# The prompt's pick transposes traced among the unsplit u tiles, and one more tile left unsplit

## The chip, the cores and the metric

The kernel runs on one core of a Trainium2 chip. The metric is the device time of one execution in microseconds (us), the lower the better; a version is timed in several runs and its median is compared. Three runs of the kernel before gave 1762.54, 1763.51 and 1766.21 us.

## What is computed

The program is one layer of an encoder for 384 tokens: 128 sample tokens (row tile 0) and 256 prompt tokens (row tiles 1 and 2). The change lies in its last part, a mixture of 16384 tiny experts with product keys:

```python
q = (hb @ w_pq).reshape(PEER_BLOCK, PEER_HEADS, 2, PEER_DHALF)
s = jnp.einsum('nhpd,hpkd->nhpk', q, peer_keys).astype(jnp.float32)
s1, i1 = lax.top_k(s[:, :, 0], PEER_TOPK)
s2, i2 = lax.top_k(s[:, :, 1], PEER_TOPK)
cand = s1[..., :, None] + s2[..., None, :]          # 16 x 16 candidates a head
sc, j = lax.top_k(cand, PEER_TOPK)
e = jnp.take_along_axis(cidx, j, axis=-1)           # cidx = i1 * 128 + i2
g = jax.nn.softmax(sc, axis=-1)
act = jax.nn.gelu(jnp.einsum('nhkd,nd->nhk', peer_u[e], hb))
return jnp.einsum('nhk,nhkd->nd', (g * act), peer_v[e])
```

So every token picks 8 x 16 experts; for each it needs the dot product with a row of `peer_u`, a gelu, the softmax weight `g`, and the sum of rows of `peer_v`.

## The kernel before

The experts are done in two ways. The sample tokens (tile 0) go the sparse way: `peer_sparse` is a Python generator of 128 steps, called *pulls* here. A pull gathers one row of u and v for each token by an indirect DMA that GpSimd issues (L1573, 1 MB into one of `EB` = 3 ring buffers `raw`), takes the dot product on VectorE (L1580), the gelu and the weight on ScalarE (L1581, L1582, `dots`), and adds the v row on VectorE (L1586, `acc`). The prompt tokens (tiles 1 and 2, 256 columns) go the dense way: all 16384 experts in 128 tiles of 128, `dense_u(j)` for gelu(u h) and later `dense_v(j)` for the sum over v. Between the two, `weights(i, T, step)` builds the dense weight matrix from one-hot products (`oh`, L1401, L1448, L1452) out of the picks of tile i and multiplies it into the gelus `G`.

`peer_select(i)` finds the picks. TensorE multiplies with the keys (`dx<-keysT,qp`) into two PSUM banks named `dx`; ScalarE copies to `psc` (L1310). VectorE does the rest: a first stage of maxima, indices and replacements on `psc` (L1314 to L1318), a second on the 80 candidates `pcd` (L1334 to L1338), then bf16 one-hots `poh` (L1358 to L1364) whose sums are the two index tables `pix`, one reduction (L1365) for each half and each four heads; the softmax weights are `pg`. For tiles 1 and 2 the function ends with three TensorE transposes (L1384) of `pix` half 0, `pix` half 1 and `pg` into a `dx` bank, and a ScalarE copy to `pT` (L1386). `weights` starts from `pT`.

A u tile is 128 x 1024 f32 by 256 columns. The first `N1` = 40 tiles are *unsplit*: eight f32 matmuls each (`fx<-h2f,w` and `mm<-h2f,w`, even and odd tiles in the PSUM banks `fx` and `mm`), straight from the loaded tile, with no other engine before them. The later tiles are *split* into two fp32r halves, `wh` by ScalarE (L230) and `wl` by VectorE (L234), and take 24 shorter matmuls (`fx<-h2h,wh` and so on). Up to tile 75 each result goes to `G`.

The program is traced in Python order: selections of tile 0, then tiles 1 and 2, then the unsplit tiles with a half pull for each from tile `S0` = 30 on, then split tiles, weights, and v tiles. A scheduler reorders this and fixes one order for each engine before the run; on the chip each engine works through its list in that order and waits where an operand isn't there. PSUM banks and SBUF buffers rotate by tag (`PSB`: `mm`, `fx`, `dx` two banks, `bx`, `cp` one), so an instruction also waits for the readers of the buffer that it takes over; the tiles of `weights` and the split halves lie in memory that the selection's tiles held. The banks `bx` and `cp` serve the RWKV pairs far ahead and the weights' products later; in between they are free.

Of the kernel before, what the change touches and what calls it, by code (L numbers as in the profile page):

```python
# [176 lines left out]
ORDER = "GGIggggR1R23DMMMGRMRDMRGMGMRMDGMMRRMGDMMMGGGMGGM"  # L177


N1, NW, NA, NB = 40, 76, 8, 24  # L180
SR, UR = (0.5, 0.5, 0.62), 0.5
S0, PH = 30, 4
OFF = [j for j in range(NW, 128) if (j - NW + 1) * NB // (128 - NW) > (j - NW) * NB // (128 - NW)]
# [12 lines left out]
class K:  # L196
# [1099 lines left out]
    def peer_select(self, i, h0=0, nh=8):  # L1296

        nc = self.nc
# [4 lines left out]
        for hb in range(0, nh, 4):  # L1303
            for half in range(2):
                pr = slice(64 * half, 64 * half + 64)
                p = self.ps([128, 4, 128], tag="dx")
# [44 lines left out]
        idx = self.t([128, 2, 8, 16], tag="pix", bufs=2)[:, :, :nh]  # L1351
# [15 lines left out]
        gw = self.t([128, nh, 16], tag=f"pg{i}{h0}", pool=self.pool if i else self.hpool2)  # L1367
# [6 lines left out]
        gw = gw.rearrange("p a b -> p (a b)")  # L1374
# [4 lines left out]
            nc.vector.tensor_copy(e, ef.rearrange("p h k -> p (h k)"))  # L1379
            return e, gw  # L1380

        p = self.ps([128, 3, 128], tag="dx")
        for q, src in enumerate((idx[:, 0].rearrange("p h k -> p (h k)"), idx[:, 1].rearrange("p h k -> p (h k)"), gw)):
            nc.tensor.transpose(p[:, q], src, self.ident)  # L1384
        T = self.t([128, 3, 128], tag=f"pT{i}", pool=self.hpool2)
# [85 lines left out]
    def dense_u(self, j):  # L1471

        nc = self.nc
        u = self.expert(self.I["puT"][j].rearrange("p k e -> p (k e)"))
        p = self.ps([128, 256], tag="mm" if j < N1 and j % 2 else "u")
        if j < N1:
            u = u.rearrange("p (k e) -> p k e", k=8)
            for k in range(8):
                self.mm(p, u[:, k], self.h2f[:, k], start=(k == 0), stop=(k == 7))
        else:  # L1480
            uh, ul = (x.rearrange("p (k e) -> p k e", k=8) for x in self.split(u, UENG[j % len(UENG)]))
            hi, lo = self.h2p
            for k in range(8):
                self.mm(p, uh[:, k], hi[:, k], start=(k == 0), stop=False)
                self.mm(p, uh[:, k], lo[:, k], start=False, stop=False)
                self.mm(p, ul[:, k], hi[:, k], start=False, stop=(k == 7))
        off = j in OFF
        g = self.G[:, j] if j < NW else self.t([128, 256], tag="gO" if off else "gA", bufs=2 if off else NA, pool=self.late)
        nc.scalar.activation(g, p, AF.Gelu_apprx_tanh)
        if off:  # L1490
            nc.sync.dma_start(self.Ad[OFF.index(j)], g)
        return g
# [97 lines left out]
    def run(self):  # L1590
# [68 lines left out]
        T = [None] + [self.peer_select(i) for i in (1, 2)]  # L1659
# [9 lines left out]
        def pull(rate):  # L1669
            sn[0] += rate  # L1670
            while sn[0] >= 1:
                sn[0] -= 1
                next(sparse, None)

        gs, todo = {}, AHEAD + [j for j in range(NW, 128) if j not in AHEAD]
        for j in range(N1):
            self.dense_u(j)
            if j >= S0:
                pull(SR[0])

        self.h2p = [self.t([128, 8, 256], F32R, tag=f"h2{x}", pool=self.peer) for x in "hl"]
        self.hilo(*self.h2p, self.h2f, eng="v")
# [15 lines left out]
        with ExitStack() as s:  # L1698
# [3 lines left out]
            nc = self.nc  # L1702
# [10 lines left out]
        for n, j in enumerate(order):  # L1713
            self.pace = self.vdone[n - 5] if n > 4 else None
            pull(SR[2])
            while todo and sum(u not in OFF for u in gs) < NA - 1:
                u = todo.pop(0)
# [37 lines left out]
```

## Time and profile before

| what | value |
|---|---|
| three timed runs | 1762.54 to 1766.21 us, median 1763.51 us |
| the profiled execution's own time | 1759.49 us |
| its span, first to last instruction | 1757.7 us |
| TensorE matmul busy | 1679.5 us (96%) |
| VectorE busy | 1353.6 us (77%) |
| ScalarE busy | 747.5 us (43%) |
| GpSimd busy | 550.5 us (31%) |
| mean granted TensorE clock | 0.981 |

The profile is one execution recorded by the chip. PE is TensorE, PEld its weight loads, DVE VectorE, ACT ScalarE, POOL GpSimd, SP the engine that issues most loads. A row of the timeline has the start, the duration, the engine and line, the operation, output and inputs, how many, and in brackets the idle time of the engine just before it with what ended that idle time. An unsplit tile's eight f32 matmuls show as 16 records. Durations of neighbours overlap a little, so the distance from start to start is what an instruction takes of its engine.

### The profile page before, as it was taken

What the parts mean: (1) busy time and instruction counts of PE and PEld (TensorE: products, weight loads), DVE (VectorE), ACT (ScalarE), POOL (GpSimd) and SP (SyncE); (2) the same over time, 40 slices, a digit from 0 to 9 for tenths busy, and PEclk for the clock granted to TensorE, in tenths of its full rate; (3) what the DMA queues carried; (4) which work ended last, traced back from release to release, by engine and by line L of the source; (5) the groups of instructions that cost most, each with busy time, mean ns of one, the idle gap of its engine ahead of it and who ended that gap; (6) DMA issues with size and microseconds to landing.
All of it is one profiled execution on the core that took longest, in us unless ns stands there. A gap on an engine that the chain in (4) does not pass through costs nothing.

```text
span 1757.7 us, 33129 instructions
## 1 busy us (share of the span) xinstructions
PE 1679.5 (96%) x12392; PEld 1410.2 (80%) x12392; DVE 1353.6 (77%) x2907; ACT 747.5 (43%) x1666; POOL 550.5 (31%) x616
## 2 busy tenths in 40 slices
PE   6999899999999999999998999999999999999998
PEld 4988788777888877899887889999976667767766
DVE  4448878778867765556999998899957778778787
ACT  4533343334342333335323255578853433443344
POOL 2433343333333421024032233342243224323232
PEclk8999899999999999999999999999999999999999
DMA  8543662555365365765488999997569999999996
GB/s 305 161 123 101 187 194 68 145 166 174 94 197 161 94 207 189 246 193 171 144 334 313 358 333 366 397 340 238 179 251 381 348 346 376 375 349 391 349 379 216
DMA packets 172537, 436.71 MB, mean 248 GB/s; under 512 B 46036, under 2 KB 86100, under 8 KB 155992
## 3 DMA queue, kind: packets, MB, share of 16 engines
q1 hardware_dynamic: 153944, 300.36, 50.8%
q0 software_dynamic: 18432, 134.23, 19.7%
q8 instruction: 98, 1.61, 0.4%
q14 instruction: 63, 0.52, 0.1%
HBM read 403.23 MB, written 31.30 MB: 247 GB/s over the span
## 4 chain that ended last, share of the span: by engine, by line
PE 55%; DVE 19%; DMA 11%; issue 8%; ACT 3%; POOL 2%; SPq 1%; DVEq 0%; POOLq 0%; ACTq 0%
PE mm L226 21%; PE fx L226 10%; PE dx L226 10%; PE cp L226 6%; PE bx L226 6%; DMA raw<-in_puv,pe 3%; DVE wl L234 3%; DVE raw L1580 2%; DVE acc L1586 2%; DMA w<-in_puT 2%; DMA w<-in_pv 2%; ACT wh L230 1%; DMA w<-in_w_in 1%; DVE TX L698 1%; DMA NL<-d 1%
## 5 line engine op out<-in xcount | busy, mean ns | idle before, releaser
L234 DVE TENSOR_TENSOR wl<-w,wh 128x1024 fp32r<-128x1024 f32 (+1 forms) x276 | 345.8, 1260 | 109.0 <-ACT wh L230 71.3
L230 ACT ACTIVATE wh<-w 128x1024 fp32r<-128x1024 f32 (+1 forms) x284 | 296.6, 1050 | 163.7 <-PE mm L226 74.3
L1573 POOL DMA_INDIRECT raw<-in_puv,pe x128 | 173.6, 1356 | 423.4 <-PE dx L226 155.4
L226 PE MATMUL fx<-h2h,wl 128*128 128x256 f32 x704 | 200.1, 285 | 8.2 <-DVE wl L234 8.0
L226 PE MATMUL fx<-h2h,wh 128*128 128x256 f32 x704 | 200.6, 285 | 1.4 <-ACT wh L230 1.1
L226 PE MATMUL fx<-h2l,wh 128*128 128x256 f32 x704 | 197.4, 281 | 0.0
L1586 DVE SCALAR_TENSOR_TENSOR acc<-raw,dots,acc 128x1024 f32<-128x1024 f32 x127 | 166.1, 1308 | 14.8 <-ACT dots L1582 14.8
L1580 DVE SCALAR_TENSOR_TENSOR raw<-raw,sh 128x1024 f32<-128x1024 f32 x128 | 158.9, 1241 | 14.0 <-DMA raw<-in_puv,pe 13.8
L226 PEld LDWEIGHTS fx<-h2h,wl 128*128 128x128 f32 x704 | 132.7, 189 | 12.3 <-DVE wl L234 11.5
L226 PEld LDWEIGHTS fx<-h2h,wh 128*128 128x128 f32 x704 | 132.6, 188 | 6.4 <-ACT wh L230 3.6
L226 PEld LDWEIGHTS fx<-h2l,wh 128*128 128x128 f32 x704 | 132.9, 189 | 1.6 <-issue 1.1
L226 PE MATMUL mm<-LTh,wh 128*128 128x384 f32 (+2 forms) x352 | 123.4, 351 | 1.4 <-ACT wh L230 0.8
L226 PE MATMUL mm<-LTl,wh 128*128 128x384 f32 (+2 forms) x352 | 123.1, 350 | 0.9 <-POOL LTl L488 0.9
L226 PE MATMUL mm<-LTh,wl 128*128 128x384 f32 (+2 forms) x352 | 122.4, 348 | 0.0
L226 PE MATMUL mm<-h2f,w 128*128 128x256 f32 x448 | 104.0, 385 | 0.0
L226 PE MATMUL mm<-wh,LTh 128*128 128x256 f32 x336 | 100.3, 299 | 2.9 <-ACT qx L888 2.9
L1581 ACT ACTIVATE dots<-dots 128x1 f32<-128x1 f32 x128 | 25.6, 200 | 177.0 <-DVE raw L1580 176.5
L226 PE MATMUL mm<-wl,LTh 128*128 128x256 f32 x336 | 99.4, 296 | 0.0
L226 PE MATMUL mm<-wh,LTl 128*128 128x256 f32 x336 | 98.6, 293 | 0.0
L226 PEld LDWEIGHTS mm<-h2f,w 128*128 128x128 f32 x448 | 85.0, 192 | 12.2 <-issue 0.2
L226 PE MATMUL fx<-h2f,w 128*128 128x256 f32 x320 | 73.8, 383 | 0.0
L226 PEld LDWEIGHTS mm<-LTh,wh 128*128 128x128 f32 (+2 forms) x352 | 66.5, 189 | 7.1 <-issue 3.0
(577 smaller groups left out, 4235.0 us busy)
## 6 DMA issues: line engine op xcount, KB each, us to landing
w<-in_puT SPq DMA_DIRECT2D x128, 512.0 KB, 7.1
w<-in_pv SPq DMA_DIRECT2D x128, 512.0 KB, 6.6
w<-in_w_in SPq DMA_DIRECT2D x70, 512.0 KB, 4.5
w<-in_w_ada SPq DMA_DIRECT2D x48, 512.0 KB, 4.8
cKT<-in_cKT SPq DMA_DIRECT2D x32, 256.0 KB, 4.3
cV<-in_cV SPq DMA_DIRECT2D x32, 256.0 KB, 4.5
w<-in_w_pq SPq DMA_DIRECT2D x16, 512.0 KB, 4.2
d<-wst SPq DMA_DIRECT2D x8, 832.0 KB, 4.3
```

The lines of the kernel that those rows point to most:

```text
L226: return self.nc.tensor.matmul(out, l, r, start=start, stop=stop, skip_group_check=True, **kw)
L230: self.nc.scalar.activation(hi, src, AF.Copy)
L234: (self.nc.vector if eng == "v" else self.nc.gpsimd).tensor_tensor(lo, src, hi, op=OP.subtract)
L698: nc.vector.tensor_tensor(X[:, :t, :t], T[:, :t, :t].rearrange("p s c -> p c s"), NL[:, :t, t].unsqueeze(1).to_broadcast([48, t, t]), op=O ...
L1573: d = nc.gpsimd.indirect_dma_start(out=bass.AP(tensor=u.tensor, offset=u.offset, ap=[u.ap[0], [1, 2048]]), out_offset=None, in_=self.I["puv"],
L1580: nc.vector.scalar_tensor_tensor(u, u, 1.0, h2, op0=OP.mult, op1=OP.mult, accum_out=dot)
L1581: nc.scalar.activation(dot, dot, AF.Gelu_apprx_tanh)
L1586: nc.vector.scalar_tensor_tensor(acc, v, dot, acc, op0=OP.mult, op1=OP.add)
```

## The change

The three transposes and the copy to `pT` leave `peer_select`, which now returns the picks, and become a function `turn`, which puts them into the bank `bx` for tile 1 and `cp` for tile 2. `run` traces `turn` behind the 21st unsplit tile (j = 20) and behind the 40th (j = 39), and `issue_after` orders each of its TensorE instructions behind that tile's last matmul, which sets the earliest place and not the place itself. `N1` becomes 41.

```diff
-N1, NW, NA, NB = 40, 76, 8, 24
+N1, NW, NA, NB = 41, 76, 8, 24
+TURNS = (20, 39)
...
-        p = self.ps([128, 3, 128], tag="dx")
+        return idx, gw
+
+    def turn(self, i, idx, gw):
+
+        nc = self.nc
+        p = self.ps([128, 3, 128], tag=("bx", "cp")[i - 1])
         for q, src in enumerate((idx[:, 0].rearrange("p h k -> p (h k)"), idx[:, 1].rearrange("p h k -> p (h k)"), gw)):
             nc.tensor.transpose(p[:, q], src, self.ident)
         T = self.t([128, 3, 128], tag=f"pT{i}", pool=self.hpool2)
...
             for k in range(8):
-                self.mm(p, u[:, k], self.h2f[:, k], start=(k == 0), stop=(k == 7))
+                self.ulast = self.mm(p, u[:, k], self.h2f[:, k], start=(k == 0), stop=(k == 7))
...
             self.dense_u(j)
             if j >= S0:
                 pull(SR[0])
+            if j in TURNS:
+                with self.tc.issue_after(self.ulast.ins):
+                    i = TURNS.index(j) + 1
+                    T[i] = self.turn(i, *T[i])
```

Lines of the changed file are one to ten higher than those of before (L1384 becomes L1390, L1580 L1586, L1586 L1592, L226 L227).

First place: TensorE where the picks of tile 1 are transposed. Before, the first transpose stands inside the 18th unsplit tile (j = 17), and tile 2's first key products behind it, in the same banks `dx`.

```order
4111 L226 MATMUL mm_11495<-h2f_9800,w_11493 128x256 x8
4112 L226 MATMUL fx_11507<-h2f_9800,w_11505 128x256 x8
4113 L226 MATMUL mm_11519<-h2f_9800,w_11517 128x256 x5
4114 L1384 MATMUL dx_11061<-cfirst,pix_11023 128x128
4115 L226 MATMUL dx_11069<-keysT_9801,qp_9803 128x128 x4
4116 L226 MATMUL mm_11519<-h2f_9800,w_11517 128x256 x3
```

In the changed program it stands one matmul before the end of the 25th tile (j = 24), and the other two behind the 29th.

```order
4125 L227 MATMUL mm_11585<-h2f_9800,w_11583 128x256 x8
4126 L227 MATMUL fx_11597<-h2f_9800,w_11595 128x256 x7
4127 L1390 MATMUL bx_11553<-cfirst,pix_11023 128x128
4128 L227 MATMUL fx_11597<-h2f_9800,w_11595 128x256
4129 L227 MATMUL mm_11609<-h2f_9800,w_11607 128x256 x8
4130 L227 MATMUL fx_11621<-h2f_9800,w_11619 128x256 x8
4131 L227 MATMUL mm_11633<-h2f_9800,w_11631 128x256 x8
4132 L227 MATMUL fx_11645<-h2f_9800,w_11643 128x256 x8
4133 L1390 MATMUL bx_11553<-cfirst,pix_11023 128x128
4134 L1390 MATMUL bx_11553<-cfirst,pg_2169_11054 128x128
```

The 16 key products of tile 2 no longer follow a transpose; they now stand in the third and fourth unsplit tile (j = 2 and 3).

Second place: VectorE where the second stage of tile 1's selection begins (`pja`, `pc`, from `pcd`). In the changed program the first stage of tile 2 (`psv<-psc`) starts between its instructions; before, all of tile 2's first stage stood behind tile 1's last reductions to `pix`.

```order
1544 L1336 MAX_INDEX pja_10964<-pfv_10963,pcd_10959 128x8
1545 L1337 MATCH_REPLACE pc_2154_10971<-pfv_10963,pcd_10959 128x80
1546 L1336 MAX_INDEX pja_10964<-pfv_10963,pcd_10959 128x8
1547 L1315 MAX psv_11061<-psc_11068 128x8 x2
1548 L1336 MAX_INDEX pja_10964<-pfv_10963,pcd_10959 128x8
1549 L1315 MAX psv_11061<-psc_11068 128x8
```

From a common point (the last `pix` reduction of tile 0) to the first-half reductions of tile 1's `pix`, 7 pulls stand on VectorE before, and 12 in the changed program, along with all of tile 2's first stage.

Third place: VectorE from the last `pix` reduction of tile 2 to the first instruction of the weights (the CAST to `wA`). Before:

```order
1764 L1365 TENSOR_REDUCE pix_11259<-poh_11283 128x64
1765 L1586 SCALAR_TENSOR_TENSOR acc_11699<-raw_13330,dots_13332,acc_11699 128x1024
1766 L1580 SCALAR_TENSOR_TENSOR raw_13397,dots_13399<-raw_13397,sh_2290_11697 128x1024
1767 L1586 SCALAR_TENSOR_TENSOR acc_11699<-raw_13397,dots_13399,acc_11699 128x1024
1768 L1424 CAST wA_13126<-pT_2172_11065 128x128
```

In the changed program:

```order
1781 L1366 TENSOR_REDUCE pix_11253<-poh_11277 128x64
1782 L1586 SCALAR_TENSOR_TENSOR raw_13243,dots_13245<-raw_13243,sh_2288_11691 128x1024
1783 L1592 SCALAR_TENSOR_TENSOR acc_11693<-raw_13243,dots_13245,acc_11693 128x1024
1784 L1586 SCALAR_TENSOR_TENSOR raw_13310,dots_13312<-raw_13310,sh_2288_11691 128x1024
1785 L1592 SCALAR_TENSOR_TENSOR acc_11693<-raw_13310,dots_13312,acc_11693 128x1024
1786 L1586 SCALAR_TENSOR_TENSOR raw_13377,dots_13379<-raw_13377,sh_2288_11691 128x1024
1787 L1592 SCALAR_TENSOR_TENSOR acc_11693<-raw_13377,dots_13379,acc_11693 128x1024
1788 L1586 SCALAR_TENSOR_TENSOR raw_13450,dots_13452<-raw_13450,sh_2288_11691 128x1024
1789 L1592 SCALAR_TENSOR_TENSOR acc_11693<-raw_13450,dots_13452,acc_11693 128x1024
1790 L1430 CAST wA_13106<-pT_2265_11557 128x128
```

Four whole pulls now stand there in a row, dot product and accumulation of each side by side, where one and a half stood. On TensorE the transposes of tile 2's picks stand behind the 40th tile, with the 41st behind them and then the first split tiles and one-hot products in almost the order of before. From there to the end the lists of the five engines differ only by instructions that move a few places.

## The prediction

> **What bounds the kernel now.** I read first who waits for whom around the transposes, from the last selection to the first split tile.
>
> ```profile
> PE dx L1384 <- DVE pix L1365: 6.8, 2, 4.9
> ```
>
> TensorE waits twice for VectorE's picks, 6.8 us in all. The timeline of TensorE shows where.
>
> ```profile
> 894.27 3.62 PE L226 MATMUL mm<-h2f,w 128*128 128x256 f32 x16
> 897.72 3.62 PE L226 MATMUL fx<-h2f,w 128*128 128x256 f32 x16
> ...
> 935.71 2.32 PE L226 MATMUL mm<-h2f,w 128*128 128x256 f32 x10
> 942.90 0.45 PE L1384 MATMUL dx<-cfirst,pix 128*128 128x128 f32 x1 [4.87 <-DVE pix L1365]
> ...
> 1012.98 0.30 PE L1384 MATMUL dx<-cfirst,pix 128*128 128x128 f32 x1 [1.95 <-DVE pix L1365]
> ...
> 1030.72 1.13 PE L226 MATMUL mm<-oh 128*128 128x128 f32 x8
> ...
> 1035.31 0.39 PE L226 MATMUL fx<-h2h,wl 128*128 128x256 f32 x1 [1.42 <-DVE wl L234]
> ```
>
> An unsplit tile takes 3.45 us, start to start. TensorE stands 4.87 us for tile 1's picks and 1.95 us for tile 2's, has all 40 tiles at 1030.7, does twelve one-hot products, and waits 1.42 us for the first split half `wl`, so VectorE is late there too. The windows say how full both engines are (columns: length, then PE, PEld, DVE, ACT and POOL busy, granted clock, DMA share, GB/s).
>
> ```profile
> 900.00:940.00 40.00, 38.03 (x177) 33.15 (x175) 38.96 (x145) 11.66 (x32) 11.25 (x10) 1.00 0.95 372
> 940.00:980.00 40.00, 37.10 (x171) 31.76 (x172) 40.00 (x147) 11.43 (x33) 12.60 (x10) 0.91 0.78 287
> 980.00:1020.00 40.00, 38.05 (x177) 33.25 (x176) 39.81 (x141) 14.19 (x35) 10.27 (x9) 1.00 0.98 370
> ...
> 1080.00:1100.00 20.00, 19.73 (x167) 19.52 (x167) 17.14 (x18) 10.65 (x22) 6.51 (x4) 1.00 0.99 379
> ```
>
> From 900 to 1020 VectorE is busy for 118.8 of 120 us. It is the bound of this stage; the unsplit tiles are filling for TensorE, and its waits are what the filling lacks. In the later window TensorE is the fuller one (19.73 of 20 against 17.14): a delay of TensorE there goes through to the end.
>
> **The change part by part.** *The first transposes.* They are to wait less because they stand 7 1/4 tiles later. But the order shows that what they wait for moves as well: the banks `dx` being free, all of tile 2's first stage and five more pulls now stand on VectorE ahead of tile 1's first-half picks.
>
> ```profile
> 900.04 1.28 DVE L1586 SCALAR_TENSOR_TENSOR acc<-raw,dots,acc 128x1024 f32<-128x1024 f32 x1
> ...
> 909.71 1.23 DVE L1580 SCALAR_TENSOR_TENSOR raw<-raw,sh 128x1024 f32<-128x1024 f32 x1 [0.54 <-DMA raw<-in_puv,pe]
> ...
> 941.69 1.06 DVE L1365 TENSOR_REDUCE pix<-poh 128x64 f32<-128x256 bf16 x2
> 942.66 0.69 DVE L1360 TENSOR_TENSOR poh<-pjb,ioe 128x1024 bf16<-128x1024 bf16 x1
> ...
> 950.18 0.87 DVE L1314 MAX8 psv<-psc 128x8 f32<-128x128 f32 x4
> ...
> 987.26 0.28 DVE L1320 CAST psf<-psi 128x256 f32<-128x256 uint32 x1
> ...
> 1019.72 1.08 DVE L1365 TENSOR_REDUCE pix<-poh 128x64 f32<-128x256 bf16 x2
> 1020.71 1.28 DVE L1586 SCALAR_TENSOR_TENSOR acc<-raw,dots,acc 128x1024 f32<-128x1024 f32 x1
> 1021.91 1.22 DVE L1580 SCALAR_TENSOR_TENSOR raw<-raw,sh 128x1024 f32<-128x1024 f32 x1
> 1023.05 0.09 DVE L1580 DVE_READ_ACCUMULATOR raw<-raw,sh 128x1 f32 x1
> 1023.74 1.28 DVE L1586 SCALAR_TENSOR_TENSOR acc<-raw,dots,acc 128x1024 f32<-128x1024 f32 x1 [0.60 <-ACT dots L1582]
> 1024.94 0.22 DVE L1424 CAST wA<-pT 128x128 uint32<-128x128 f32 x1
> ...
> 1034.03 1.23 DVE L234 TENSOR_TENSOR wl<-w,wh 128x1024 fp32r<-128x1024 f32 x1
> 1035.17 0.69 DVE L1401 TENSOR_TENSOR oh<-wA,wB 128x512 f32<-128x512 f32 x1
> ```
>
> A pull costs VectorE 1.14 (1021.91 to 1023.05) and 1.20 us (1020.71 to 1021.91), 2.34 together. Tile 2's first stage, with the eight maxima behind it, runs from 950.18 to 987.26, 37.1 us; seven pulls (16.4) and one half of a pair of reductions (0.5) lie in it, and 20 us are its own. So the picks come 20 + 5 x 2.34 = 31.7 us later than at 942.66, at 974.4. To that come waits. With three ring buffers, a pull's gather starts only when the accumulation three pulls ahead has ended: the one at 900.04 ended at 901.24, and the dot product that it held up started at 909.71, 8.5 us on. In the new order two pulls of this stretch have only some 7 us of VectorE's work in that place, which makes waits of about 1.3 and 0.7, and 0.4 come from places that already wait a little. The picks come at 976.8.
>
> TensorE stood at 938.03 (935.71 + 2.32) before its wait. To the new place it has 7 1/4 tiles x 3.45 = 25.0 us and the sixteen key products, 0.2 us each by this row, 3.2:
>
> ```profile
> 875.09 1.26 PE L226 MATMUL dx<-keysT,qp 64*128 64x128 f32 x12
> ```
>
> It is there at 966.2 and waits 10.6 us, not 4.87. No gain here, a loss of 5.7, bounded by 3.5 (no wait for gathers) and 8 (gathers at their slowest, below).
>
> *The clock.* A long wait also costs what follows it.
>
> ```profile
> 942.90:944.00 1.10, 1.10 (x4) 0.50 0.83 149
> ...
> 948.00:950.00 2.00, 2.00 (x7) 0.59 0.55 94
> 950.00:952.00 2.00, 2.00 (x11) 1.00 0.96 399
> ```
>
> Behind the 4.87 us the granted clock is 0.50 until about 949.6, 6.7 us at half speed, 3.4 us lost; behind the 1.95 us TensorE runs on at full speed. The change keeps one such stretch: nil for the difference. [...]
>
> *The second transposes.* From 976.8 TensorE has 15 1/8 tiles (52.2), 3.4 for the clock and about 0.7 for six transposes, and reaches tile 2's at about 1033. VectorE's order up to the last `pix` has two dot products and one accumulation less than before (-3.5) and the waits of above (+2.4), so it is through at 1020.7 - 1.1 = 1019.6. The wait of 1.95 us goes, and nothing is late in its place on TensorE.
>
> *The pulls behind them.* What was left out of the way comes here: four whole pulls in a row ahead of the weights' CAST, where one and a half stood. Their own work is 9.4 us. With nothing between dot product and accumulation each accumulation waits for ScalarE, 0.7 us (1023.05 to 1023.74), 2.8 in all. And the ring holds three: the third pull's gather starts with an accumulation that ends at about 1018.2 and is there 8.5 us later, at 1026.7, where VectorE is ready at 1025.7 (wait 1.0); the fourth's starts at 1022.6 and is there at 1031.1, where VectorE is ready at 1029.7 (1.4). The CAST comes at 1019.6 + 9.4 + 2.8 + 2.4 = 1034.2, not 1024.94. Nothing hides this: the CAST is what the first one-hot products and `wl` are queued behind. TensorE's second transposes, which the CAST also has to follow (its tiles lie where the picks lay), are through by then.
>
> ```profile
> DMA to landing us min/median/max: 5.7/8.7/10.7
> ```
>
> The gathers took 5.7 to 10.7 us from issue to landing between 895 and 1035. At the one end both waits of the burst go (-2.4), at the other it grows by about 4; I take the lag of 8.5, which was measured where VectorE waited for it.
>
> *The seam.* From the CAST to the end of the first `wl` VectorE took 10.2 us (1024.94 to 1035.17); one dot product and one one-hot product now stand later, so 8.5. The first `wl` is there at 1042.7 instead of 1035.17, 7.5 us later. TensorE then has one tile more behind it. A split tile takes 24 matmuls, and two of the next are done ahead; by the later window above (20 us for 167) a matmul takes 0.12 us, so that is 2.8 + 0.2 = 3.0 us. TensorE is 7.5 - 3.0 = 4.5 us behind the old program. VectorE has one pull (2.34) and one `wl` (1.14) more behind it and one one-hot product (about 0.6, the row at 1035.17 less its overlap) less: 7.5 - 2.9 = 4.6 behind. Both are late by the same amount, so neither covers the other. That the 41st tile takes 3.45 us unsplit instead of 2.8 is paid inside this.
>
> *What is regained.*
>
> ```profile
> PE fx L226 <- DVE wl L234: 4.3, 6, 1.6
> ```
>
> From 1035 to 1160 TensorE waits 4.3 us for `wl`, 1.42 of them at the seam. The other 2.9 could shrink; VectorE is just as late and keeps its order, so I take back 0.5.
>
> **Sum.** +4.5 - 0.5 = +4.0 us. The profiled execution took 1759.49 us, 1.8 outside its span of 1757.7; it would take 1763.5. It lies 4.0 under the median of the three runs, 1763.51, whose counterpart is 1767.5. 0.2% (3.5 us) is about what a measurement of this kernel can tell from no change, and the forecast lies just above it.
>
> **The rivals.** *The delay is regained.* VectorE has idle time behind the seam (2.9 us in 1080 to 1100 alone), so it catches up, and TensorE's later waits of 2.9 us go. For it: those waits are VectorE's. Against it: TensorE has 0.3 us idle in that window and cannot catch up itself. +1 to +2.5 us, about 1765.
>
> *The mixed selections pack better (the other side).* Where an instruction needs the one before it, VectorE loses a little; with two selections mixed, the one can fill the other's gaps. If tile 2's first stage and tile 1's second together take 6 us less than summed here, the first picks come at 971, TensorE's second transposes and the CAST at about 1028, the first `wl` at 1036.5, 1.3 later than before with 3.0 us more done; with VectorE ahead the 2.9 us of later waits go too, and the gain is 4.6: 1758.9. It decides at first picks before about 972. Against it: the two reductions at 941.69 take 0.97 us to the next row's start though one row says 1.06 for them, so neighbours overlap already, and VectorE was idle for 1.2 of 120 us.
>
> *The gathers of the burst are slow.* At 10.7 us from the end of an accumulation, the third and fourth pull wait 2.2 us more each; the DMA share is 0.98 there already. +7 to +9, about 1771.
>
> *The change doesn't do what it says.* The transposes of tile 1 don't stand behind the 21st tile but in the 25th and behind the 29th; the scheduler's list is fixed, so this is in the forecast and no case of its own.
>
> **How the numbers follow.** Forecast (+1.5 to +6.5) 0.56, of which 0.33 lies above 3.5; regained 0.17; better packed 0.15, nearly all of it as a gain over 0.2%; slow gathers 0.12. Slower 0.33 + 0.12 = 0.45, faster 0.14, the rest, 0.41, within 0.2%. The range leaves out half of the gain and the end of the slow gathers: 1760.0 to 1772.0.
>
> **What would show it.** Right: in the changed profile TensorE waits some 10 us for `pix` near 966, the clock is at 0.50 behind it, there is no wait at the second transposes, VectorE's `acc` rows wait for `dots` and `raw` rows for DMA four times between 1019 and 1034, and the first `wl` ends near 1042. Wrong: a first wait under 6 us, a CAST before 1029, or a first `wl` as late as forecast with the end no later, which would say that the stages behind give the time back.

## The result and the profile after

The changed kernel takes 1777.55 us (median of 8 runs, 1770.12 to 1784.62), the kernel before on the same chip 1764.86 us (8 runs, 1760.62 to 1770.69). The ratio is 1.0068, with an interval of 1.0045 to 1.0090: 12.0 us slower, 7.9 to 15.9. The forecast was 4.0 us slower, in a range that ended at 1772.0.

One execution of either program can't be set against the other as it stands. The profiled execution after spans 1780.5 us and the one before 1757.7, and 5.3 of these 22.8 us are there before anything differs: up to the first key product of the selections each engine has the same list in both. So I count from that product. TensorE's timeline of before gives it and the first product of the v tiles, VectorE's the CAST that starts tile 2's weights (the *second CAST* from here on).

```profile
836.33 0.72 PE L226 MATMUL dx<-keysT,qp 64*128 64x128 f32 x8
...
1223.78 0.22 DVE L1424 CAST wA<-pT 128x128 uint32<-128x128 f32 x1
...
1288.52 2.81 PE L226 MATMUL bx<-w,G 128*128 128x512 f32 x6
```

The same three rows after:

```profile
841.66 0.72 PE L227 MATMUL dx<-keysT,qp 64*128 64x128 f32 x8
...
1237.79 0.23 DVE L1430 CAST wA<-pT 128x128 uint32<-128x128 f32 x1
...
1303.77 2.81 PE L227 MATMUL bx<-w,G 128*128 128x512 f32 x6 [0.86 <-ACT wst L1420]
```

The second CAST comes 387.5 us behind the first key product before and 396.1 after (+8.7), the first v tile 452.2 and 462.1 (+9.9). That is nearly the measured 12.0. The v tiles took 7.5 us more in this execution than in the one of before; I don't count them, since single executions don't show how much of that, if any, the change causes (run 18 below).

TensorE's timeline after, at the places that the prediction named:

```profile
958.10 5.41 PE L227 MATMUL fx<-h2f,w 128*128 128x256 f32 x16 [2.87 <-ACT G L1495]
...
980.83 0.33 PE L1390 MATMUL bx<-cfirst,pix 128*128 128x128 f32 x1 [3.94 <-DVE pix L1366]
...
1035.14 0.38 PE L1390 MATMUL cp<-cfirst,pix 128*128 128x128 f32 x2
1035.36 0.27 PE L1390 MATMUL cp<-cfirst,pg 128*128 128x128 f32 x1
1035.47 3.62 PE L227 MATMUL fx<-h2f,w 128*128 128x256 f32 x16
1044.63 0.58 PE L227 MATMUL fx<-h2h,wh 128*128 128x256 f32 x1 [5.54 <-ACT wh L231]
...
1046.13 2.08 PE L227 MATMUL mm<-oh 128*128 128x128 f32 x8 [0.70 <-DVE oh L1407]
...
1051.11 0.37 PE L227 MATMUL fx<-h2h,wl 128*128 128x256 f32 x1
```

The picks of tile 1 are still waited for, 3.94 us, and 2.87 us went shortly ahead of that, on a gelu. The second transposes don't wait. But then TensorE stands 5.54 us for the first split half, and this time for `wh`, ScalarE's, and 0.70 us more for the first one-hots; for `wl` it doesn't wait. VectorE's timeline after shows the pulls ahead of the weights:

```profile
1023.34 1.08 DVE L1366 TENSOR_REDUCE pix<-poh 128x64 f32<-128x256 bf16 x2
...
1026.16 1.28 DVE L1592 SCALAR_TENSOR_TENSOR acc<-raw,dots,acc 128x1024 f32<-128x1024 f32 x1 [0.60 <-ACT dots L1588]
1029.06 1.23 DVE L1586 SCALAR_TENSOR_TENSOR raw<-raw,sh 128x1024 f32<-128x1024 f32 x1 [1.62 <-DMA raw<-in_puv,pe]
...
1032.86 1.23 DVE L1586 SCALAR_TENSOR_TENSOR raw<-raw,sh 128x1024 f32<-128x1024 f32 x1 [0.68 <-DMA raw<-in_puv,pe]
...
1037.41 1.23 DVE L1586 SCALAR_TENSOR_TENSOR raw<-raw,sh 128x1024 f32<-128x1024 f32 x1 [1.43 <-DMA raw<-in_puv,pe]
...
1040.44 0.22 DVE L1430 CAST wA<-pT 128x128 uint32<-128x128 f32 x1
...
1041.57 1.22 DVE L1586 SCALAR_TENSOR_TENSOR raw<-raw,sh 128x1024 f32<-128x1024 f32 x1
...
1047.79 2.35 DVE L235 TENSOR_TENSOR wl<-w,wh 128x1024 fp32r<-128x1024 f32 x2
```

Four pulls stand there, their gathers waited for with 3.7 us in all, and the CAST is at 1040.44. ScalarE's timeline after says why `wh` is late: it stands in ScalarE's list behind the `dots` of the pull at 1041.57.

```profile
1042.83 0.20 ACT L1587 ACTIVATE dots<-dots 128x1 f32<-128x1 f32 x1 [2.97 <-DVE raw L1586]
...
1043.53 1.04 ACT L231 ACTIVATE wh<-w 128x1024 fp32r<-128x1024 f32 x1
```

The windows of TensorE around the restart (length, PE busy, granted clock, DMA share, GB/s):

```profile
1044.63:1045.63 1.00, 0.79 (x2) 0.50 1.05 438
...
1049.63:1050.63 1.00, 1.00 (x7) 0.58 0.83 311
1050.63:1051.63 1.00, 1.00 (x11) 1.00 1.06 434
```

For the first 6 us behind the wait TensorE runs at half speed, so it reaches the first matmul on `wl` at 1051.11 though `wl` was there at about 1049.0.

Last, the rest of the weights in windows (length, then PE, PEld, DVE, ACT and POOL busy, clock, DMA share, GB/s): from 300 us behind the first key product to the second CAST, and on to the first v tile. Before:

```profile
1136.33:1223.78 87.45, 85.76 (x732) 84.56 (x731) 85.98 (x111) 65.03 (x166) 31.36 (x22) 1.00 0.85 305
1223.78:1288.52 64.74, 62.55 (x535) 61.35 (x534) 59.45 (x92) 55.67 (x154) 15.92 (x17) 1.00 0.52 177
```

After:

```profile
1141.66:1237.79 96.13, 91.76 (x780) 89.76 (x780) 93.27 (x117) 69.43 (x175) 29.40 (x24) 1.00 0.84 303
1237.79:1303.77 65.98, 61.78 (x520) 60.95 (x519) 56.96 (x92) 56.04 (x155) 16.58 (x17) 0.97 0.50 170
```

TensorE is idle for 4.4 and 4.2 us there, for 1.7 and 2.2 before, and the clock dips in the last stretch. Nothing of the delay is regained behind the seam; some is added.

### The profile page after: what moved, and what is told of

Same layout as the page of the kernel before. It is cut to its first block, busy times and chain, and to the rows that moved or that the text cites. A ratio compares the mean times of both kernels' runs of the same rounds, so it can differ in the third digit from the quotient of the medians.

```text
span 1780.5 us, 33120 instructions
## 1 busy us (share of the span) xinstructions
PE 1684.8 (95%) x12384; PEld 1413.3 (79%) x12384; DVE 1353.7 (76%) x2906; ACT 745.3 (42%) x1665; POOL 529.8 (30%) x616
## 4 chain that ended last, share of the span: by engine, by line
PE 49%; DVE 21%; DMA 14%; issue 9%; ACT 4%; POOL 2%; SPq 0%; DVEq 0%; ACTq 0%; POOLq 0%
PE mm L227 20%; PE fx L227 11%; PE dx L227 8%; PE cp L227 5%; PE bx L227 5%; DMA raw<-in_puv,pe 4%; DVE wl L235 3%; DVE raw L1586 3%; DMA w<-in_pv 2%; DVE acc L1592 2%; ACT wh L231 2%; DMA w<-in_w_in 2%; DMA w<-in_puT 1%; DMA NL<-d 1%; DMA w<-in_w_ada 1%
## 5 line engine op out<-in xcount | busy, mean ns | idle before, releaser
L1579 POOL DMA_INDIRECT raw<-in_puv,pe x128 | 163.4, 1277 | 449.8 <-PE dx L227 166.0
L227 PE MATMUL fx<-h2h,wl 128*128 128x256 f32 x696 | 198.8, 286 | 9.1 <-DVE wl L235 9.0
L227 PE MATMUL fx<-h2h,wh 128*128 128x256 f32 x696 | 198.8, 286 | 8.3 <-ACT wh L231 8.3
L227 PE MATMUL fx<-h2l,wh 128*128 128x256 f32 x696 | 195.8, 281 | 0.0
L1592 DVE SCALAR_TENSOR_TENSOR acc<-raw,dots,acc 128x1024 f32<-128x1024 f32 x127 | 166.2, 1309 | 16.7 <-ACT dots L1588 16.6
L1586 DVE SCALAR_TENSOR_TENSOR raw<-raw,sh 128x1024 f32<-128x1024 f32 x128 | 160.3, 1253 | 18.3 <-DMA raw<-in_puv,pe 18.2
L227 PEld LDWEIGHTS fx<-h2h,wh 128*128 128x128 f32 x696 | 132.0, 190 | 14.1 <-ACT wh L231 12.4
L227 PEld LDWEIGHTS fx<-h2h,wl 128*128 128x128 f32 x696 | 132.3, 190 | 13.4 <-DVE wl L235 12.7
L227 PEld LDWEIGHTS fx<-h2l,wh 128*128 128x128 f32 x696 | 132.1, 190 | 1.3 <-issue 0.9
L227 PE MATMUL mm<-LTh,wh 128*128 128x384 f32 (+2 forms) x352 | 124.2, 353 | 1.8 <-ACT pt L504 1.0
L227 PE MATMUL mm<-LTl,wh 128*128 128x384 f32 (+2 forms) x352 | 123.5, 351 | 0.7 <-POOL LTl L489 0.7
L227 PE MATMUL mm<-LTh,wl 128*128 128x384 f32 (+2 forms) x352 | 122.8, 349 | 0.0
L227 PE MATMUL mm<-h2f,w 128*128 128x256 f32 x448 | 103.7, 385 | 0.0
L227 PE MATMUL mm<-wh,LTh 128*128 128x256 f32 x336 | 99.6, 297 | 2.9 <-ACT qx L889 2.9
L227 PE MATMUL mm<-wl,LTh 128*128 128x256 f32 x336 | 98.8, 294 | 0.0
L227 PE MATMUL mm<-wh,LTl 128*128 128x256 f32 x336 | 98.1, 292 | 0.0
L227 PEld LDWEIGHTS mm<-h2f,w 128*128 128x128 f32 x448 | 85.6, 193 | 12.5
L227 PE MATMUL fx<-h2f,w 128*128 128x256 f32 x336 | 78.5, 386 | 2.9 <-ACT G L1495 2.9
L227 PEld LDWEIGHTS fx<-h2f,w 128*128 128x128 f32 x336 | 64.6, 194 | 12.5 <-ACT G L1495 3.3
```

Source lines behind the costliest of these rows:

```text
L227: return self.nc.tensor.matmul(out, l, r, start=start, stop=stop, skip_group_check=True, **kw)
L1579: d = nc.gpsimd.indirect_dma_start(out=bass.AP(tensor=u.tensor, offset=u.offset, ap=[u.ap[0], [1, 2048]]), out_offset=None, in_=self.I["puv"],
L1586: nc.vector.scalar_tensor_tensor(u, u, 1.0, h2, op0=OP.mult, op1=OP.mult, accum_out=dot)
L1592: nc.vector.scalar_tensor_tensor(acc, v, dot, acc, op0=OP.mult, op1=OP.add)
```

## The experiments

Every run was timed beside the kernel before on the same chip. Times below are the difference from that kernel, with its 95% interval in brackets (the ratio and its interval, less one, times the median of before). No run leaves work out.

**First: the parts of the change.** I took the place of the second transposes as the cause (T): behind the 40th tile they hold back the CAST, since the weights' tiles lie where the picks lay, and the scheduler fills the gap with pulls. Rivals were the 41st tile (N) and the mixing of the two selections (I).

*1, the tile alone.*

```diff
-N1, NW, NA, NB = 40, 76, 8, 24
+N1, NW, NA, NB = 41, 76, 8, 24
```

> Edit: the kernel before with one number changed, 41 unsplit u tiles for 40; the transposes stay in the dx banks and in their old place. Theory T (the place of the second transposes costs the time: behind the 40th tile they hold back the CAST, and four whole pulls run ahead of it): the extra tile only fills a wait of 1.4 us at the seam and saves 1.1 us of VectorE, so -2 to +1 us against before. Rival N (the extra unsplit tile costs the time, 3.45 us against 2.8 and all behind it): +4 to +12 us. Rival I (tile 2's first stage ahead of tile 1's picks costs the time): -2 to +1 us as with T, since the old order stays.

+0.9 us (-2.5 to +4.2). N falls.

*2, the transposes alone.* The changed kernel with `N1` = 40.

> Edit: the changed kernel with 40 unsplit tiles for 41, the transposes behind the 21st and the 40th tile as changed. In VectorE's order three pulls stand ahead of the CAST behind the last picks, and two split halves ahead of the one-hot products. T: most of the loss stays, +7 to +13 us against before, with TensorE waiting 5 us or more for the first split tile and the clock at 0.5 behind it. N: 0 (-2 to +2). I: +8 to +12, from a wait of 4 to 10 us at the first transposes.

+8.1 us (4.8 to 11.5). Most of the loss is there without the tile.

*3, the banks alone.* In the kernel before:

```diff
-        p = self.ps([128, 3, 128], tag="dx")
+        p = self.ps([128, 3, 128], tag=("bx", "cp")[i - 1])
```

> Edit: the kernel before with nothing but the banks of the two transposes changed (bx for tile 1, cp for tile 2); they are traced in the selection as before, 40 unsplit tiles. The order mixes the two selections as in the changed kernel (first transposes of tile 1 in the 25th tile), but tile 2's stand behind the 34th and 36th tile and only one pull stands between the last picks and the CAST. T: no loss, -4 to +2 us against before, the CAST at 1022 to 1028. I: most of the loss, +6 to +12 us. N: 0.

+14.5 us (9.9 to 19.1): T as the only cause falls. The CAST did come early, 4.9 us sooner than before. But more pulls and one-hots stand between it and the first `wl`, and TensorE, one tile short, waits for that:

```profile
1039.06 0.58 PE L226 MATMUL fx<-h2h,wl 128*128 128x256 f32 x1 [3.79 <-DVE wl L234]
```

*4, the second transposes early.*

```diff
-TURNS = (20, 39)
+TURNS = (20, 34)
```

> Edit: the changed kernel with the second transposes behind the 35th tile for the 40th, 41 unsplit tiles. VectorE's order up to the last picks is that of the changed kernel, behind them one pull stands ahead of the CAST for four. T: the CAST comes some 8 to 10 us sooner than in the changed kernel and the loss is gone, -4 to +2 us against before. I and N: it stays, +8 to +12 us.

+4.1 us (1.1 to 7.1). Two thirds of the loss are gone, though not all of it as T wanted, and the 41st tile covers the wait that the third run met. TensorE's timeline has, at the second transposes and at the first split half:

```profile
1017.12 0.33 PE L1390 MATMUL cp<-cfirst,pix 128*128 128x128 f32 x1 [2.63 <-DVE pix L1366]
...
1040.67 0.39 PE L227 MATMUL fx<-h2h,wh 128*128 128x256 f32 x1 [0.34 <-ACT wh L231]
```

**Second: what lies behind.** I set side by side the lists that the scheduler wrote for the last 32 groups of one-hot products, far behind the transposes. Runs 1 and 4 have the list of before, to the row; runs 2 and 3 and the changed kernel have others. So run 4 undoes two things at once, the late second transposes and the new list. TensorE's end of it, with O1 for one group of four one-hot products and s7 for seven split matmuls, is before, and in the changed kernel:

```
O1 s8 O1 s1 O1 s13 O7 V3 O1
O3 s24 O1 s4 O1 s2 O1 s10 O1 s1 O7 s2 O1 V3 O1
```

So theory O: a part of the loss is that order.

*5, another list with the old front.* In the kernel before:

```diff
-S0, PH = 30, 4
+S0, PH = 28, 4
```

> Edit: the kernel before with one number changed, S0 = 28 for 30, so that the pulls are traced from two tiles earlier. Transposes, banks and 40 tiles are those of before, and VectorE's order is the same up to the first split halves; but behind the second CAST of the weights the scheduler lists the one-hots and split halves of tile 2 in the other way that it also chose for the run with 40 tiles and late transposes. Theory O (some 5 us of the loss come from that list, far behind the transposes): +3 to +7 us against before, with TensorE idle for 8 us instead of 4 from 300 us behind the first key product to the first v tile. Rival S (all of the loss comes from the picks and the seam): -1.5 to +1.5 us.

+8.3 us (4.8 to 12.0), from one number that leaves transposes, banks and the list up to the first split halves alone. That excludes S. But its v tiles are listed otherwise, too, so which of the later lists costs the time this run doesn't say. TensorE is idle for 5.2 us in the stretch behind the second CAST, 2.2 before, at a clock of 0.97:

```profile
1229.15:1295.73 66.58, 61.43 (x514) 60.56 (x513) 57.69 (x92) 54.88 (x152) 15.45 (x17) 0.97 0.50 169
```

*6, the first transposes later.* `TURNS = (28, 39)` in the changed kernel.

> Edit: the changed kernel with the first transposes behind the 29th tile for the 21st; all of VectorE's order stays. The wait of 3.9 us at them should go, and with it the half clock behind it. Theory D (VectorE sets the stage, so TensorE only waits that much longer at the first split tile, 9 to 12 us for 5.5): the loss stays, +10 to +13 us against before. Rival W (the wait at the first transposes is a part of the loss): +4 to +8 us.

+11.5 us (7.2 to 15.7), the loss of the change. The wait I meant to remove stayed, at the later place:

```profile
989.50 0.48 PE L1390 MATMUL bx<-cfirst,pix 128*128 128x128 f32 x1 [6.50 <-DVE pix L1366]
...
1038.07 0.47 PE L227 MATMUL fx<-h2h,wh 128*128 128x256 f32 x1 [4.24 <-ACT wh L231]
```

It grew by 2.6 and the wait at the seam shrank by 1.3. So D's time came but not its wait there (4.24 us for 9 to 12). W isn't tried by this, but between these two places that of the first transposes doesn't matter.

*7, both later and earlier.* `TURNS = (28, 36)`.

> Edit: the changed kernel with the transposes behind the 29th and the 37th tile, 41 unsplit tiles. Two pulls stand between the last picks and the CAST for four, and the one-hots behind the second CAST end as in the kernel before. Theory T+O (the place of the second transposes and the list of the last one-hots cost the time, the mixing of the selections nothing): -4 to +2 us against before, the CAST some 5 to 8 us sooner than in the changed kernel. Rival I (the mixing costs it): +8 to +12 us.

+3.5 us (0.0 to 6.9), as run 4: an early second turn takes most of the loss away, with the selections mixed as in the changed kernel. I as the main cause falls.

*8, one tile more.* `N1` = 42 in the changed kernel.

> Edit: the changed kernel with 42 unsplit tiles for 41. The four pulls and the list behind the second CAST stay. The extra tile fills 3.45 us of TensorE's wait of 5.5 us for the first split tile. Theory C (a part of the loss at the seam is the half clock behind that wait, 3.3 us): with a wait of about 2 us the clock stays at 1.00, so +5 to +9 us against before, 3 to 5 us less than the changed kernel. Rival V (VectorE alone sets the seam): +10 to +13 us, as the changed kernel.

+7.4 us (3.9 to 10.9), 4.6 less than the change, though the two intervals overlap. TensorE's timeline, at the first one-hots and at the first split half:

```profile
1042.47 1.78 PE L227 MATMUL mm<-oh 128*128 128x128 f32 x8 [2.70 <-DVE oh L1407]
...
1047.65 0.38 PE L227 MATMUL fx<-h2h,wh 128*128 128x256 f32 x1 [0.39 <-ACT wh L231]
```

The 6.2 us of waits are 3.1, and the half speed behind them lasts some 3.5 us instead of 6. C has its time, but the clock did not stay at 1.00 as C wanted.

**Third: the list held.** The order of before is written into the kernel as a list of names, and each instruction is ordered behind the one ahead of it on its engine; that sets places only and adds no wait for a semaphore.

```diff
+        for s in LISTS:
+            s = [self.seq[k] for k in s.split()]
+            for m, prev in zip(s[1:], s):
+                self.tc.add_manual_dep(m.ins, prev.ins.name, mybir.DependencyInfo(
+                    mybir.DependencyClass.NoSync, mybir.DependencyReason.DATA), reason="list")
```

*9 to 12, VectorE alone held*, from the second CAST to the last product: in the changed kernel, with 42 tiles, in run 3, and with 42 tiles and `TURNS = (20, 34)`.

> Edit: the changed kernel, with one thing undone that the change did not name: behind the second CAST of the weights VectorE's one-hots, products and split halves are held in the order in which the kernel before has them (86 instructions, each listed behind the one before it; nothing waits for a semaphore that it did not wait for before). All ahead of that stays as changed, the four pulls and the wait at the seam among it. Theory O (about 8 of the 12 us come from that list, the rest from the seam): +2 to +6 us against before; second CAST to end 533 to 537 us instead of 543. Rival S (all of it comes from the picks and the seam, and the list was a chance companion): +10 to +13 us.

+10.9 us (6.7 to 15.3).

> Edit: the changed kernel with 42 unsplit tiles for 41 and with the list of before behind the second CAST. Theory O+C: both parts of the loss are cut, the list (8 us, by the run with S0 = 28) and the cold wait at the seam (4 us, by the run with 42 tiles): -1 to +2 us against before. Rival (the two overlap, since TensorE's lateness at the seam is what the list would have hidden): +4 to +7 us.

+7.6 us (3.9 to 11.5), as run 8 without the list.

> Edit: the kernel before with the transposes in bx and cp, 40 unsplit tiles, as tried above at +14 us, and with the list of before behind the second CAST. Theory O: the list is worth 7 to 8 us here too, so +4 to +8 us is left, which the waits at the picks and the first split halves must explain. Rival (the banks alone cost it): +12 to +15 us.

+5.6 us (1.6 to 9.9), 9 less than run 3.

> Edit: the changed kernel with 42 unsplit tiles, the second transposes behind the 35th tile and the list of before behind the second CAST, the version that leaves out every part found to cost something but the mixing of the two selections. Theory O+T+C: it is as fast as before or a little faster, -5 to +2 us. Rival I (the mixing itself costs 3 to 4 us, as the runs with early second transposes hint): +2 to +6 us.

+6.9 us (3.0 to 10.9): this version was meant to be as fast as before, and isn't.

As they stand these are against theory O, run 11 excepted. But with VectorE's list forced, the scheduler wrote TensorE's anew, in none of the four that of before (in run 9 it ends in ten groups of one-hot products in a row). So none of the four, run 11 included, says what the whole order of before would do.

*13 to 16, TensorE, VectorE and ScalarE held* over the same stretch, with the same rows as before on all three but for a few at the start of the stretch: S0 = 28, the changed kernel, the changed kernel with 42 tiles, and the banks alone.

> Edit: the kernel before with S0 = 28 (above at +8.3 us), and TensorE, VectorE and ScalarE held to the order that the kernel before has behind the second CAST, from there to the last product of the weights (351, 82 and 149 instructions, each listed behind the one before it on its engine, no new wait for a semaphore). Theory O (those lists cost the 8 us): -1.5 to +2.5 us against before. Rival (the lists behind the weights, or the pulls themselves, cost it): +5 to +10 us.

+5.6 us (2.5 to 8.8), where run 5 had 8.3: in the rival's range, not in O's.

> Edit: the changed kernel with the three engines held to the order of before behind the second CAST; all ahead of it as changed. Theory O (two thirds of the loss are those lists, one third the seam): +2 to +6 us against before. Rival S (the loss is made ahead of the second CAST and only kept behind it): +9 to +13 us.

+3.7 us (-0.9 to +8.3), where the change has 12.0: in O's range.

> Edit: the changed kernel with 42 unsplit tiles and the three engines held to the order of before behind the second CAST. Theory O+C: -1 to +3 us against before. Rival S: as with 42 tiles alone, +5 to +9 us.

+2.8 us (-0.4 to +5.8), where run 8 has 7.4: in O's range too, though the two intervals overlap.

> Edit: the kernel before with the transposes in bx and cp and 40 tiles (above at +14.5 us), the three engines held to the order of before behind the second CAST. Theory O: +3 to +7 us against before, as with VectorE alone held (+5.7) or a little less. Rival (VectorE's list was not the cause there): +12 to +16 us.

+12.5 us (8.1 to 16.9), where run 3 has 14.5: against O. In runs 13 and 16 the lists of the v tiles behind came out far from those of before, in runs 14 and 15 nearly the same, which the last two runs take up.

*17 and 18, the rest.* Run 3 with all five engines held from the second CAST to the end; the changed kernel with all five held from the v tiles on, and its own order of the last weights.

> Edit: the kernel before with the transposes in bx and cp, 40 tiles (+14.5 us alone, +12.5 with three engines held over the last weights), and all five engines held to the order of before from the second CAST to the end of the program. Theory O2 (the order of the v tiles counts as well as that of the last weights): +2 to +6 us against before, what the picks and the seam cost. Rival (the order behind the second CAST is not what costs it): +10 to +15 us.

+6.7 us (2.8 to 10.6), a little over O2's figure.

> Edit: the changed kernel with all five engines held to the order of before from the first v tiles to the end; the last weights keep the order of the changed kernel. Theory O2: the v tiles are about half of what the order costs, so +6 to +9 us against before, with 3 to 4 us still lost between the second CAST and the first v tile. Rival 1 (the last weights alone): +10 to +13. Rival 2 (the v tiles alone): +2 to +5.

+12.7 us (8.1 to 17.5): nothing gained. In the changed kernel it is the last weights, rival 1. Runs 14 and 18 differ in hardly more than the order of these, and the windows from the second CAST to the first v tile show it, run 14 first:

```profile
1230.64:1293.36 62.72, 60.55 (x519) 59.35 (x517) 58.97 (x92) 54.70 (x153) 15.74 (x17) 1.00 0.51 179
```

```profile
1235.17:1300.65 65.48, 60.45 (x520) 59.46 (x519) 58.37 (x92) 56.07 (x155) 15.83 (x17) 1.00 0.50 171
```

2.2 us idle against 5.0. Over all twenty kernels this stretch takes 62.7 to 64.7 us in the eight that have TensorE's list of before there, and 65.4 to 68.2 in the twelve that have another: about 3 us on average, with no overlap. It does not order the kernels by their time, though: run 7 takes 67.0 us there and loses 3.5 in all, run 16 takes 63.4 and loses 12.5. The timed difference of runs 14 and 18 is 9.0, give or take 6.6 (the half widths 4.6 and 4.7 put together as independent), so more than 3 us is neither shown nor excluded. And run 18, with the v tiles listed as before, takes 476.1 us from the first of them to the end (1776.7 of span less 1300.65), as the changed kernel does (476.7) and not as the one execution of before (469.2): the order of the v tiles doesn't make that length. Whether the order of the last weights has a part in it isn't settled: runs 6 and 8, which have it too, take 475.1 and 471.4 us there, runs 14 and 15, with the order of before, 474.0 and 468.5, one execution each.

## Why the prediction was wrong, point by point

Times of after are given here less 5.3 us, to stand beside the prediction's.

The first picks: forecast 976.8, they came at 975.5 (980.83). TensorE got there at 976.89 (980.83 less its wait of 3.94), so at 971.6, where 966.2 was forecast: 5.4 later, of which 2.87 are the wait for a gelu, which I had not foreseen, and 1.8 the half speed behind it (5.41 us for a tile of 3.62). So it waited 3.94 us and not 10.6, and a first wait under 6 us was one of the signs of being wrong that I had named. That VectorE is the bound of this stage was right all the same, as run 6 shows: moving the first transposes moves the wait and not the time.

The second transposes: no wait, as forecast; the last `pix` ends at 1019.1, forecast 1019.6.

The pulls: the CAST came at 1035.1, forecast 1034.2. The gathers were waited for with 3.7 us instead of 2.4, three times and not twice. The term was right in its sum, 0.9 short.

**The seam** failed in size. TensorE's delay at the first `wl` is 10.5 us and less the 3.0 us of work done ahead 7.5, where I had 4.5. The first `wl` ended at about 1043.7, forecast 1042.7, which is 1.0 of the 3.0 that were missing. The other 2.1: TensorE took it up only at 1045.8. It had stood 5.54 us, a wait of that length cost the clock here, and at half speed it was late through the work that stands ahead of the first `wl`. I charged one stretch at half speed at the picks and none at the seam. Yet by my own figures TensorE was through with the 41st tile at about 1036.8 (1033, three transposes and a tile of 3.45) and had some 3.3 us of work for the 5.9 us up to 1042.7, so a wait was in them. I had also not looked on ScalarE's list for `wh`, which stands there behind the `dots` of a pull; but this matters less, since the first one-hots, of VectorE, were waited for as well, until 1046.13 in the changed kernel's own time. Run 8, with 42 tiles, halves the waits (5.54 and 0.70 us become 2.70 and 0.39) and nearly the half speed, and its time fell by 4.6 us, which by itself isn't clear of its interval.

**"What is regained ... keeps its order, so I take back 0.5"** is the step that failed in kind. VectorE's order behind the seam was not kept, nor was TensorE's; the rows of the order that I read ended at the seam. I had written that from there to the end the lists differ only by instructions that move a few places, and priced that at nothing; in the last weights such moves are what costs. Up to the second CAST the delay is 8.7, not 4.0: 7.5 at the seam and 1.2 lost behind it, where 0.5 was to be regained. What cost these 1.2 isn't shown. Behind the second CAST the order of the last weights costs about 3 us by the rows (65.98 us in the changed kernel, 62.72 in run 14), and timed, holding it to the order of before leaves +3.7 of the +12.0, while run 18, which keeps the new order there, has +12.7. The kernel, being late, has fewer matmuls left in that stretch (519 in run 14, 535 before) and would have come through it 2.0 us faster than before (62.72 against 64.74), so only 1.2 of the 3 shows between +8.7 and the +9.9 at the first v tile. Together 4.0 + 3.0 (the seam) + 1.7 (1.2 lost up to the second CAST instead of 0.5 regained) + 1.2 gives the 9.9 of the rows; the measured 12.0 has it well inside its interval.

The rivals: none had this mechanism. *Slow gathers* came nearest in time, but the gathers were only 1.3 us slower than forecast. *Regained* and *packed better* are excluded by the rows: the delay is +8.7 and +9.9 behind the seam, and the first picks came at 975.5, not before 972. What *packed better* starts from, that VectorE loses a little where an instruction needs the one before it, is small in the profile before: of two instructions of 0.29 us, L1349 starts 0.33 us behind the L1348 whose `pst` it reads (932.27 and 932.60), and the `acc` row that needs neither starts 0.21 us behind L1349 (932.81).

What stays open: where the part of the 9.0 us between runs 14 and 18 lies that is more than the 3 of the rows, if there is one; why S0 = 28 with the list held is still 5.6 us slower than before, and why the banks alone lost 12.5 with the last weights held and 6.7 with all the rest held. Their v tiles are listed otherwise, and the intervals of 12.5 and 6.7 overlap, so that the order of the v tiles costs something there is argued, not shown. No version tried is faster than before; the 41st tile alone is as fast.

## What to carry to other kernels

Where a scheduler writes a list for each engine from simulated times, a small edit rewrites lists far behind it, and that can cost as much as the edit itself: compare the order to the end of the program, not to the end of the stage. Before an edit is called slow, hold the rest of the program to the old order, on all engines at once (one engine alone makes the others' lists new), and time again. And a wait that a sum moves to another place can cost a stretch at half speed there, as the 5.54 us at the seam cost some 6 us of it here: price it where the wait will be.

## What the runs showed of the hardware

The waits of TensorE and its clock behind them. Behind the 1.95 us at 1012.98 in the kernel before, the clock stayed at 1.00. Behind 2.87 us it was at half for about 3.4 us, here in windows of 1 us from the changed kernel's restart at 958.10:

```profile
958.20:959.20 1.00, 1.00 (x3) 0.56 0.86 348
959.20:960.20 1.00, 1.00 (x3) 0.50 1.10 373
...
961.20:962.20 1.00, 1.00 (x5) 0.74 0.98 410
962.20:963.20 1.00, 1.00 (x7) 1.00 0.86 238
```

The 2.70 us of run 8 and the 2.63 us of run 4 did the same: in windows of 1 us the clock was 0.57, 0.50, 0.50, 0.72 and then 1.00 from 1042.63 in run 8, and 0.74, 0.50, 0.50, 0.55 from 1017.50 in run 4. But the length of the wait alone doesn't decide it: 1.98 us lowered the clock in run 5, and 3.77 us didn't in run 12. Run 5's TensorE timeline and its window of 1 us, 2 us behind the restart, and then the same of run 12:

```profile
1016.73 0.30 PE L1384 MATMUL dx<-cfirst,pix 128*128 128x128 f32 x1 [1.98 <-DVE pix L1365]
...
1018.83:1019.83 1.00, 1.00 (x4) 0.50 1.03 418
```

```profile
973.29 0.33 PE L1392 MATMUL bx<-cfirst,pix 128*128 128x128 f32 x1 [3.77 <-DVE pix L1368]
...
975.00:976.00 1.00, 1.00 (x6) 1.00 0.92 361
```

What decides between the two, these rows don't show. How long the clock stayed at half, and from when, the profiles before and after show for 890 to 1060 us. In the changed kernel it was from 958.31 to 961.73 (3.4 us) behind the wait of 2.87 us that ended at 958.10, from 982.21 to 985.62 (3.4 us) behind the 3.94 us that ended at 980.83, and from 1043.65 to 1050.47 (6.8 us) with the 5.54 us that ended at 1044.63. In the kernel before it was from 942.81 to 949.63 (6.8 us) with the 4.87 us that ended at 942.90. The clock fell 0.21 and 1.38 us behind the restart in the first two, 0.98 and 0.09 us ahead of it in the others. Behind the 5.54 us there is a second gap of 0.70 us in the restart, behind the 4.87 us there is none; why half speed lasted twice as long behind these two isn't shown.

Executions of one program lie far apart: the kernel before took 1753.00 to 1773.54 us in the runs made beside these experiments, so two profiles of one execution each differ by 20 us at worst with no cause in the program. Much of that arises early: the first key product, up to which VectorE, ScalarE and GpSimd have the same list in all twenty kernels, came at 832.7 to 843.7 us.
